# Hybrid encoder block on one core: the gated memory operand made in the values stage, small steps in PSUM, and another split of the last eight units

## The chip, the core and the metric

The kernel runs on one core of one Trainium2 chip. Its time is the device time of one execution in microseconds (us). A core has a matrix engine (TensorE, PE in the profile; PEld is its load of weights), VectorE (DVE), ScalarE (ACT), GpSimd (POOL) and SyncE (SP), which here only issues transfers between DRAM and the on-chip memory SBUF. TensorE writes its results into PSUM, a small memory of banks.

## The reference

One encoder block on 1024 tokens of width 1024, in float32. The input is normalised and multiplied by one wide matrix; its columns feed three mixers and their gates. Cut to what matters:

```python
h = rms_norm(x, g_pre)
a_qkv, bq, bk, bv, mq, ga, gb, gm, mg = split(h @ w_in)
# a: dilated window attention in three groups (windows 128, 512, 2048; dilations 1, 4, 16), 8 heads of 64 each
wts = softmax(stack(lses), axis=0)               # shares of the three groups, by their log-denominators
oa = einsum('gbsh,gbshd->bshd', wts, stack(outs))
# b: grouped attention, RMS-normalised queries and keys, rotary positions on two axes
# m: cross-attention into 256 rows of memory
om = softmax(mq @ km.T * M_HEAD_DIM ** -0.5) @ vm
ya = (oa * silu(ga)) @ w_br_a
yb = (ob * silu(gb)) @ w_br_b
ym = (om * silu(gm)) @ w_br_m
gates = sigmoid(mg + b_merge)
merged = gates[0] * ya + gates[1] * yb + gates[2] * ym
x = x + rms_norm(merged @ w_out, g_post)
```

"Operand" below means `o * silu(g)`, the left factor of one of the three branch products: 512 channels by 1024 tokens, kept as four blocks k of 128 channels, each in two halves of 512 tokens (`lo`, `hi`, `half[z]`).

## The kernel before

**Precision.** Every float32 operand of a product is split into a high part (a rounded copy, by ScalarE) and a low part (the difference, by VectorE or GpSimd); a product is then three matmuls, high·high, low·high and high·low. The helper `split` is at L105 (ScalarE's copy) and L106 (VectorE's difference). So every product needs a step of each engine ahead of it.

**Seven products for eight.** Most large products are cut into two by two blocks and made by seven block products with sums of blocks. The names A11, A12, S2, S1, S4, S3, A22 are blocks and sums on the weights' side, T1 to T4 on the tokens' side. The sum S2 needs A-blocks, S4 needs S2, S1 needs S2, and each is split before its product.

**Order of work.** Every engine runs its instructions in the order in which the program gives them; a wait holds what stands behind it on the same engine. Transfers nearly all stand in SyncE's queue in program order, so that one that waits (a store for its data, a load for its tile to come free) holds those behind it. A pool hands out tiles by name; a name with `bufs=1` has one buffer, and a new use waits for the old one's last reader.

The stages in order of time, in us of the profiled execution:

- up to 220: keys and values of the memory, attention into it. Its result o goes to `od[2]` in DRAM; the gates' silu, doubled, went to `g2d`.
- 220 to 460: the grouped attention.
- 462 to 538: products of the values stage (L1210). In its loop the eight blocks r of the b operand are made, by `operand(r, stage)`: stage 0 loads `vot` (from od), `vgt` (from g2d) and `vrt` (1/l from rld), stage 1 multiplies on VectorE (L992, L993), stage 2 stores back to od (L995). `vot` has two buffers, `vgt` and `vrt` have one.
- 538 to 579: the third group's values (L1259): 28 steps, product i and block k of step n being `divmod(n, 4)`, with 12 matmuls a step; the products run in the order A11, A12, S2, S3, S4, S1, A22; `SIDE` lists by step what the other engines do. Split S3 stands at step 8, S4 at 12, S1 at 16, the load of `tab` at 9. What remains of operand 7 is at step 7 of the list.
- 579 to 1062: 25 pairs of units (L1298), 18.3 us each: rotary parts, gates and merge gates. In the last two the memory operand is gated: `op_load` loads od and g2d halves, `op_mult` (L1323) multiplies, `op_split` splits into `hh`, `hl`.
- 1062 to 1297: `weave`. It takes turns between the dense units `y` (steps m = 0 to 15, L1862, 24 matmuls of 512 columns each: the branch products by 128 output channels) and the attention of the 12 dilated items; it hands a dense step out when the share of attention cost already given, against a total that is written in the call, is behind that of the dense work. `pend` holds small steps (evacuations, loads, splits) that are given every third dense step.
- 1297 to 1349: the last eight y units (`y_part`, L1995). `y_load` loads a weight, `y_split` splits it (ScalarE at L1337, second engine at L1338), `y_evac` multiplies the product by its merge gate (L1355, VectorE, out of PSUM) and adds it to the accumulator (L1356, GpSimd). `wo_split` splits parts of the output weights that `wo_load` brought, and `a_half` (L1982) halves the accumulators for the output product.
- 1349 to the end: the output product z (L2081), the norm and the sum with x.

The shares of the last item's three groups are made in `shares_3(T)`: from transposed rows (L1898) a minimum, differences, exponentials, a sum, a reciprocal and `parts` (L1901 to L1917), which TensorE transposes (L1922). `wide` spreads them over the channels, and `first_two` and `third` (L1946 to L1948) combine the groups' outputs; `dl_high` and `dl_low` split the result as operand of the a branch.

Of the kernel before, what the change touches and what calls it, by code (L numbers as in the profile page):

```python
# [15 lines left out]
S = 1024  # L16
# [34 lines left out]
def block(ctx: ExitStack, tc: tile.TileContext, x, xT, memT, cst, msk, bcst, tabA, gpost,  # L51
# [944 lines left out]

    turn = [0]
# [204 lines left out]
    for n in range(28):  # L1202
# [34 lines left out]
        if k == 3:  # L1237
# [3 lines left out]
            4: [lambda: v3_split("S2")], 5: [lambda: kt_split("T3", 0)], 6: [lambda: kt_split("T3", 1)], 7: [lambda: operand(7, 1), lambda: operand(7, 2)],  # L1241
# [6 lines left out]
            26: [lambda: k_block(0, "S2")], 27: [lambda: k_block(0, "S1"), lambda: k_block(0, "S3"), lambda: k_sum(0, 4)]}  # L1248
    for n in range(28):
# [59 lines left out]
    def op_load(t):  # L1309
        for k in range(4):  # L1310
            if t is lo and k % 2 == 0:
                x = vb.tile([P, 1024], F32, name=f"vA12{k // 2}")
                for z in range(2):
                    OPM[lo, k + z] = x[:, half[z]]
            elif t is hi and k % 2 == 0:
                x = vb.tile([P, 1024], F32, name=f"vA11{k // 2}")
                for z in range(2):
                    OPM[hi, k + z] = x[:, half[z]]
            for dst, src in ((tab[k // 2][:, half[k % 2]], g2d), (OPM[t, k], od)):
                nc.sync.dma_start(dst, src[2, k, :, t])  # L1320

    def op_mult(t, k):
        V.scalar_tensor_tensor(OPM[t, k], OPM[t, k], 0.5, tab[k // 2][:, half[k % 2]], op0=OP.mult, op1=OP.mult)  # L1323
# [23 lines left out]
    def y_evac(m, t, ps_):  # L1347
# [6 lines left out]
        else:  # L1354
            V.scalar_tensor_tensor(th[:, t], th[:, t], 1.0, ps_, op0=OP.add, op1=OP.mult)  # L1355
            (V if m == 23 else G).tensor_tensor(accs[f][:, t], accs[f][:, t], th[:, t], op=OP.add)  # L1356
# [15 lines left out]
    for n in range(last + 1):  # L1372
# [4 lines left out]
        k_block(n, "A22")  # L1377
        if n:
            c_fin(n - 1, 1, 1)
# [11 lines left out]
        if n == last:  # L1391
            op_split(lo, 2)
            op_split(lo, 3)
            op_load(hi)
            qk_first(0)
            th_load(0)
# [20 lines left out]
        if n == last:  # L1417
            for k in range(4):
                op_mult(hi, k)
            y_load(1)  # L1420
            qk_first(1)
# [13 lines left out]
        if n == last - 1:  # L1435
            for k in range(4):
                op_mult(lo, k)
# [9 lines left out]
    for k in range(4):  # L1447
        op_split(hi, k)
    r = RV[last, 0, 1]
# [15 lines left out]
    with ExitStack():  # L1465
# [218 lines left out]
        def plan(it, pre, nxt):  # L1684
# [7 lines left out]
            def tokens(T):  # L1692
# [7 lines left out]
                if n in (9, 10) and T == 5:  # L1700
                    dl_load(n - 9)
                if n == 11:
                    if T < 6:
                        k, z = divmod(T, 3)
                        dl_high(k, half[z]) if z < 2 else dl_low(k)
# [145 lines left out]
        def add_y(m):  # L1851
            n, i, f = steps[m]

            def gen(_):
                pend.extend([lambda: th_load(m + 1), lambda: y_load(m + 2), lambda: y_split(m + 1, G)])
# [38 lines left out]
        def shares_3(T):  # L1894
            if T == 0:
                C["ogs"] = [OG[3, x] for x in range(2)]
                tp = pst()
                PE.transpose(tp[:, 0, 0:64], rows, ident[0:64, 0:64])  # L1898
                V.tensor_copy(c3[:, 0:2].rearrange("p g h s t -> p (g h s t)"), tp[:, 0, 0:64])
                mn = cb.tile([P, 2, NT], F32, name="cmn", bufs=2)  # L1900
                V.tensor_tensor(mn, c3[:, 0, :, 0], c3[:, 1, :, 0], op=OP.min)  # L1901
                V.tensor_tensor(mn, mn, c3[:, 2, :, 0], op=OP.min)
                C["e"] = eg = cb.tile([P, 3, 2, NT], F32, name="ceg", bufs=1)
                V.tensor_tensor(eg, c3[:, :, :, 0], mn[:, None].to_broadcast([P, 3, 2, NT]), op=OP.subtract)
                A.activation(eg, eg, AF.Exp, scale=-1.0)
            elif T == 1:
                eg = C["e"]
                dn = cb.tile([P, 3, 2, NT], F32, name="cdn", bufs=1)
                V.tensor_tensor(dn, eg, c3[:, :, :, 1], op=OP.mult)
                ds_ = cb.tile([P, 2, NT], F32, name="cds", bufs=2)  # L1910
# [3 lines left out]
                V.scalar_tensor_tensor(eg, eg, 0.5, ds_[:, None].to_broadcast([P, 3, 2, NT]), op0=OP.mult, op1=OP.mult)  # L1914
                eg = eg.rearrange("p g h t -> p (g h t)")
                A.activation(parts[:, 0], eg, AF.Copy)
                V.tensor_tensor(parts[:, 1], eg, parts[:, 0].bitcast(F32), op=OP.subtract)  # L1917
                dl_high(2, lo)
            elif T == 2:
                dl_high(2, hi)  # L1920
# [3 lines left out]
                for x in range(2):  # L1924
# [3 lines left out]
                                    pick[:, None, :, None].to_broadcast([96, 32, NT, 2]), op=OP.mult)  # L1928
            else:
                dl_low(2)  # L1930
# [19 lines left out]
        def ending():  # L1950
            DL[3] = C["ogs"][0]
            return [(lambda: [wide(g, 0) for g in range(2)], 300.0), (lambda: [wide(g, 1) for g in range(2)], 300.0),
                    (lambda: [first_two(0), wide(2, 0)], 1000.0), (lambda: [first_two(1), wide(2, 1)], 1000.0),
                    (lambda: third(0), 1000.0), (lambda: dl_high(3, lo), 100.0), (lambda: third(1), 1000.0),
                    (lambda: dl_low(3, lo), 100.0), (lambda: dl_high(3, hi), 100.0), (lambda: dl_low(3, hi), 1000.0),
                    (out_pool, 100.0), (lambda: [wo_load(nm, k) for nm in ("B11", "B21") for k in range(4)], 500.0)]
# [40 lines left out]
    LATER = {16: [("B11", 0), ("B11", 1)], 17: [("B11", 2), ("B11", 3)], 18: [("B21", 0), ("B21", 1)],  # L1997
# [314 lines left out]
```

## Time and profile before

| | us |
|---|---|
| time, median of 3 runs | 1441.6 (1441.11 to 1445.11) |
| profiled execution | 1442.91 |
| its span | 1440.8 |
| granted TensorE clock, mean over the span | 0.989 |
| PE, DVE, ACT, POOL busy | 1393.1, 1024.4, 658.9, 620.7 |
| bytes moved by transfers | 208.10 MB, 144 GB/s in the mean |

The span is what the traces cover; the execution's time lies 2.1 us above it. In the profile, L12 is line 12 of the kernel; a row of the timeline gives start, length, engine, line, operation, tile written <- tiles read, shape, and in brackets the idle time of the engine ahead of it with what ended it. A count behind an x says that so many instructions are drawn together. PEclk is the granted TensorE clock as a share of full speed.

### The profile page before, as it was taken

Reading aid. Unit: us, or ns where it says so; the run is one execution under the profiler, and the core shown is the slowest. Engines: PE = TensorE matmul, PEld = TensorE weight load, DVE = VectorE, ACT = ScalarE, POOL = GpSimd, SP = SyncE. Lnnn points to the kernel's source line nnn. Section 1 sums busy time; section 2 is a strip of 40 time slices with the busy share of each in tenths; the row PEclk is TensorE's granted clock in tenths of the full one; section 3 lists DMA queues with packets and bytes.
Section 4 is the critical chain, followed back from the end, with each engine's and each line's share of the span. In section 5 each row is a group of like instructions: output and inputs, shape, how many; then the busy total and the mean of one; then the engine's idle time right before and its main releaser. Section 6 shows DMA issues by size and latency. Waiting matters only on the chain.

```text
span 1440.8 us, 21841 instructions
## 1 busy us (share of the span) xinstructions
PE 1393.1 (97%) x7775; PEld 1110.3 (77%) x7775; DVE 1024.4 (71%) x1801; ACT 658.9 (46%) x1384; POOL 620.7 (43%) x468
## 2 busy tenths in 40 slices
PE   7999999999999999999999999999989999978897
PEld 7799986666666889888888888888867777756786
DVE  7768578776763787776777766777776655665977
ACT  6544356665644444333333333333345665532332
POOL 1416703666664002354555544555510266374303
PEclk9999999999999999999999999999999999989999
DMA  6356432222111886243333333333384667744355
GB/s 239 96 168 235 161 121 88 96 77 94 59 50 45 283 265 215 76 132 102 117 104 117 117 116 111 104 102 100 114 283 159 198 211 198 219 142 148 134 205 175
DMA packets 119708, 208.10 MB, mean 144 GB/s; under 512 B 32336, under 2 KB 60848, under 8 KB 119600
## 3 DMA queue, kind: packets, MB, share of 16 engines
q1 hardware_dynamic: 109808, 192.69, 42.1%
q10 hardware_dynamic: 9792, 14.03, 2.7%
q8 instruction: 61, 1.00, 0.3%
q14 instruction: 47, 0.39, 0.1%
HBM read 142.38 MB, written 64.28 MB: 143 GB/s over the span
## 4 chain that ended last, share of the span: by engine, by line
PE 81%; DVE 6%; POOL 3%; ACT 3%; issue 3%; DMA 2%; ACTq 1%; SPq 1%; DVEq 0%; POOLq 0%
PE s L1298 32%; PE d L1862 4%; PE s L1210 4%; PE s L2081 4%; PE ov L797 3%; PE d L145 3%; PE d L143 3%; PE d L147 3%; PE s L1259 3%; PE s L1566 2%; PE s L782 2%; PE s L781 2%; PE tr L763 2%; PE tr L1638 2%; PE d L2081 2%
## 5 line engine op out<-in xcount | busy, mean ns | idle before, releaser
L788 POOL TENSOR_TENSOR bl<-bl,bp 128x512 f32<-128x512 f32 x96 | 130.8, 1362 | 54.3 <-ACT bp L784 48.9
L1298 PE MATMUL s<-hh,vS 128*128 128x512 f32 x400 | 133.6, 395 | 0.0
L1298 PE MATMUL s<-vA,vS 128*128 128x512 f32 x450 | 106.6, 390 | 0.0
L1579 ACT ACTIVATE pra<-pra,sts 128x192 f32<-128x192 f32 (+2 forms) x176 | 75.4, 430 | 54.5 <-DVE sts L1578 51.0
L106 DVE TENSOR_TENSOR vS<-vot,vS 128x512 fp32r<-128x512 f32 x75 | 85.8, 1145 | 19.9 <-ACT vS L105 19.9
L1298 PEld LDWEIGHTS s<-vA,vS 128*128 128x128 f32 x450 | 84.5, 188 | 18.3
L784 ACT ACTIVATE bp<-s 128x512 f32<-128x512 f32 x128 | 75.7, 595 | 43.6 <-PE s L782 42.6
L764 DVE TENSOR_REDUCE bn<-tr 128x1 f32<-128x512 f32 x128 | 84.8, 682 | 11.9 <-PE tr L763 10.7
L143 PE MATMUL d<-hh,wh 128*128 128x512 f32 x224 | 90.0, 402 | 2.4 <-DVE fth L216 2.4
L147 PE MATMUL d<-hh,wl 128*128 128x512 f32 x224 | 90.0, 402 | 0.0
L145 PE MATMUL d<-hl,wh 128*128 128x512 f32 x224 | 89.4, 399 | 0.0
L1298 PEld LDWEIGHTS s<-hh,vS 128*128 128x128 f32 x400 | 75.3, 188 | 18.3 <-DVE vS L106 0.4
L1298 PE MATMUL s<-hl,vS 128*128 128x512 f32 x200 | 79.1, 396 | 0.0
L1298 PE MATMUL s<-hh,wl 128*128 128x512 f32 x200 | 78.4, 392 | 0.0
L1298 PE MATMUL s<-hh,wh 128*128 128x512 f32 x200 | 78.4, 392 | 0.0
L1298 PE MATMUL s<-hl,wh 128*128 128x512 f32 x200 | 77.8, 389 | 0.0
L1617 DVE COPY app<-tr 128x384 f32<-128x384 f32 (+1 forms) x64 | 38.8, 607 | 47.8 <-PE tr L1605 31.4
L1302 ACT ACTIVATE vv<-s 128x512 f32<-128x512 f32 x50 | 29.9, 598 | 86.0 <-PE s L1298 58.1
L1356 POOL TENSOR_TENSOR acc<-acc,wl 128x512 f32<-128x512 f32 (+1 forms) x23 | 39.8, 1731 | 51.4 <-DVE wl L1355 51.3
L1338 POOL TENSOR_TENSOR wh<-wr,wh 128x512 fp32r<-128x512 f32 x20 | 26.1, 1303 | 80.2 <-ACT wh L1337 70.3
L797 PE MATMUL ov<-bp,VS 128*64 128x512 f32 x256 | 58.5, 599 | 0.0
L1044 POOL TENSOR_TENSOR vot<-vot,vA 128x512 f32<-128x512 f32 x12 | 19.0, 1583 | 91.1 <-DVE vS L106 91.1
(619 smaller groups left out, 4142.2 us busy)
## 6 DMA issues: line engine op xcount, KB each, us to landing
wr<-in_wu SPq DMA_DIRECT2D x40, 512.0 KB
vA<-in_wu SPq DMA_DIRECT2D x24, 512.0 KB
qkd<-ko SPq DMA_DIRECT2D x96, 128.0 KB
wl<-thd SPq DMA_DIRECT2D x24, 512.0 KB
wos<-os SPq DMA_DIRECT2D x12, 512.0 KB
wr<-in_wbr SPq DMA_DIRECT2D x24, 256.0 KB
aq<-qkd SPq DMA_DIRECT2D x12, 512.0 KB
ak<-qkd SPq DMA_DIRECT2D x12, 512.0 KB
```

The lines of the kernel that those rows point to most:

```text
L106: V.tensor_tensor(dst_l, src, dst_h.bitcast(F32), op=OP.subtract)
L143: PE.matmul(dst, wh[:, k, :], hh[k][:, t], start=k == 0, stop=False)
L145: PE.matmul(dst, wh[:, k, :], hl[k][:, t], start=False, stop=False)
L147: PE.matmul(dst, wl[:, k, :], hh[k][:, t], start=False, stop=k == 7)
L764: fp["last"] = V.tensor_reduce(st[i]["n"][:, j, c:c + 1], s, axis=AX.X, op=OP.min)
L784: A.activation(pp, s, AF.Exp, scale=-1.0)
L788: G.tensor_tensor(lsum[i % 2], lsum[i % 2], pp, op=OP.add)
L797: PE.matmul(o[e * 64:e * 64 + 64], VS[:, kt, kv], d.pop(kt), start=kt < 2, stop=kt >= NT - 2)
L1210: PE.matmul(now[j], a, b, start=k == 0 and q == 0, stop=k == 3 and q == 2)
L1298: PE.matmul(BANK[n, c], a, b, start=k == 0 and q == 0 and not more, stop=k == 3 and q == 2, skip_group_check=c in "XW")
L1579: A.activation(src, src, AF.Exp, scale=-1.0, bias=bias, accum_out=sts[:, h, 1, T:T + 1])
L2081: PE.matmul(dst[:, e[0]:e[1]], a, b, start=k == 0 and q == 0, stop=k == 3 and q == 2)
```

## The change

1. **Memory operand.** `memory_operand(k, stage)` makes the gated block k of the memory operand inside the L1259 loop and stores it back to `od[2]`. It uses two `vot`, one `vgt` and one `vrt`. Loads are at steps 3, 6, 9, 12, multiplications at 5, 8, 11, 14, stores at 6, 9, 12, 14. The rest of operand 7 moves to steps 2 and 3. `op_mult` and the loads of g2d in the last pair units go; the load of the second half moves one unit earlier.
2. **Last shares.** `shares_3` keeps its temporaries in a PSUM bank, sums the three terms with one tensor_reduce, and the splits `dl_high(2)`, `dl_low(2)` stand one call later.
3. **End of the attention.** LAST_PAD and the total of `weave` grow, and the last combination (`third`, `dl_high(3)`, `dl_low(3)`), `out_pool` and the loads of B11 and B21 move out of `weave` behind it, together with y_split 17 and 18 on VectorE. Units 16 to 18 are then done in k = 0, 1, next k = 2, next B11's splits, next k = 3.
4. **Last eight units.** For m from 16 on, the sum in `y_evac` and the low parts of `y_split` are on VectorE (before, the sum of m = 23 and the splits from 21 on only were).
5. Loads and splits of the first two dilated results come one item earlier.

```diff
+    def memory_operand(k, stage):
+        if stage == 0:
+            OT["m"] = [vb.tile([P, 512], F32, name=x, bufs=2 if x == "vot" else 1) for x in ("vot", "vot", "vgt", "vrt")]
+            for z in range(2):
+                for src, dst in ((od, OT["m"][z]), (g2d, OT["m"][2 + z])):
+                    nc.sync.dma_start(dst, src[2, k, :, half[z]])
+        elif stage == 1:
+            for z in range(2):
+                o, g = OT["m"][z::2]
+                V.scalar_tensor_tensor(o, o, 0.5, g, op0=OP.mult, op1=OP.mult)
+        else:
+            o = OT.pop("m")
+            for z in range(2):
+                nc.sync.dma_start(od[2, k, :, half[z]], o[z])
...
+    SIDE[2].append(lambda: operand(7, 1))
+    SIDE.setdefault(3, []).append(lambda: operand(7, 2))
+    for j in range(4):
+        for z in range(3):
+            at = min(3 + 3 * j + (0, 2, 3)[z], 14)
+            SIDE.setdefault(at, []).append(lambda j=j, z=z: memory_operand(j, z))
...
-            for dst, src in ((tab[k // 2][:, half[k % 2]], g2d), (OPM[t, k], od)):
-                nc.sync.dma_start(dst, src[2, k, :, t])
+            elif t is hi:
+                OPM[hi, k] = tab[k // 2][:, half[k % 2]]
+            nc.sync.dma_start(OPM[t, k], od[2, k, :, t])
-    def op_mult(t, k):
-        V.scalar_tensor_tensor(OPM[t, k], OPM[t, k], 0.5, tab[k // 2][:, half[k % 2]], op0=OP.mult, op1=OP.mult)
...
-            (V if m == 23 else G).tensor_tensor(accs[f][:, t], accs[f][:, t], th[:, t], op=OP.add)
+            (V if m >= 16 else G).tensor_tensor(accs[f][:, t], accs[f][:, t], th[:, t], op=OP.add)
...
     for k in range(4):
         op_split(hi, k)
+    y_split(1, G)
...
+                C["b"] = b = pss1()
+                b = b[:, 0:192].rearrange("p (x y) -> p x y", x=12)
+                C["e"] = eg = b[:, 4:7].rearrange("p g (h t) -> p g h t", h=2)
+                mn = b[:, 7].rearrange("p (h t) -> p h t", h=2)
...
-                V.tensor_tensor(ds_, dn[:, 0], dn[:, 1], op=OP.add)
-                V.tensor_tensor(ds_, ds_, dn[:, 2], op=OP.add)
+                V.tensor_reduce(ds_, b[:, 8:11].rearrange("p g x -> p x g"), axis=AX.X, op=OP.add)
...
-        weave(16, every(), FIRST_PAD + 12 * NT * (SOFT + 100.0) + 4 * LAST_PAD + 7000.0)
+        weave(16, every(), FIRST_PAD + 12 * NT * (SOFT + 100.0) + 4 * LAST_PAD + 8000.0)
         while pend:
             pend.pop(0)()
+        y_split(17)
+        y_split(18, V, qk.tile([P, S], R, name="aq", bufs=2))
+        y_load(19)
+        out_pool()
+        for nm in ("B11", "B21"):
+            for k in range(4):
+                wo_load(nm, k)
+        third(0)
+        dl_high(3, lo)
+        third(1)
+        dl_low(3, lo)
+        dl_high(3, hi)
+        dl_low(3, hi)
...
-    y_split(17, G)
-    y_split(18, G, yw.tile([P, 1024], R, name="yw"))
-    for m in range(16, 19):
-        y_part(m, range(3))
+    for ks in (range(2), range(2, 3)):
+        for m in range(16, 19):
+            y_part(m, ks)
+    for k in range(4):
+        wo_split("B11", k)
     for m in range(16, 24):
         y_part(m, range(3, 4) if m < 19 else range(4))
         if m > 16:
             y_evac(m - 1, slice(0, S), YP[m - 1].rearrange("p a b -> p (a b)"))
         if m in (16, 17):
-            y_split(m + 3, G)
+            y_split(m + 3)
...
-FIRST_PAD, LAST_PAD = 7000.0, 1000.0
+FIRST_PAD, LAST_PAD = 7000.0, 2000.0
```

More of the change, by code (lines that the diff above doesn't have):

```diff
@@ L1435, in block @@
         if n == last - 1:
[L1436 to L1437 removed]
+            op_load(hi)
         pair_product(n, "S4")
@@ L1951, in ending @@
             DL[3] = C["ogs"][0]
[L1952 to L1956, printed above, removed]
+            return [(lambda: [wide(g, 0) for g in range(2)], 500.0), (lambda: [wide(g, 1) for g in range(2)], 500.0),
+                    (lambda: [first_two(0), wide(2, 0)], 2500.0), (lambda: [first_two(1), wide(2, 1)], 2500.0)]
         def every():
```

64 lines of the change are left out of this document (27 added, 37 removed).

## The prediction

> **What bounds the kernel now.** I read the page from the top: totals, then slices, then the busy time of the stretches that the change touches, then the waits inside them.
>
> ```profile
> span 1440.8 us, 21841 instructions
> ...
> PE 1393.1 (97%) x7775; PEld 1110.3 (77%) x7775; DVE 1024.4 (71%) x1801; ACT 658.9 (46%) x1384; POOL 620.7 (43%) x468
> ...
> PE   7999999999999999999999999999989999978897
> ...
> PEclk9999999999999999999999999999999999989999
> ```
>
> TensorE is busy 97% of the span, and the change neither adds nor removes a matmul in quantity. Time can come only from the 48 us in which TensorE is idle and from stretches at a lower granted clock; time can be lost wherever TensorE is full today and something new makes it wait. The slices put nearly all gaps behind slice 29 (from about 1050 us on). The stretches, by windows (columns: window, its length, PE, PEld, DVE, ACT, POOL busy, granted clock, DMA share, GB/s):
>
> ```profile
> 538.60:578.70 40.10, 40.10 (x337) 40.10 (x336) 30.52 (x39) 17.55 (x29) 7.24 (x4) 1.00 0.68 213
> 1062.00:1082.00 20.00, 15.30 (x71) 10.37 (x69) 10.87 (x30) 8.39 (x23) 3.51 (x3) 0.91 0.91 323
> ...
> 1276.00:1286.00 10.00, 2.27 (x10) 1.50 (x10) 8.87 (x11) 0.93 (x4) 8.92 (x6) 0.79 0.38 131
> 1286.00:1297.00 11.00, 10.94 (x63) 8.68 (x64) 8.24 (x13) 2.29 (x4) 4.87 (x3) 0.72 0.51 165
> 1297.00:1321.00 24.00, 18.95 (x74) 14.46 (x72) 8.88 (x12) 6.39 (x12) 6.30 (x5) 0.93 0.40 132
> 1321.00:1349.00 28.00, 27.65 (x122) 22.93 (x123) 28.00 (x24) 10.02 (x19) 17.00 (x7) 1.00 0.50 170
> 1349.00:1362.00 13.00, 8.56 (x28) 6.33 (x27) 12.90 (x13) 1.79 (x4) 4.08 (x2) 0.74 0.24 83
> ```
>
> The first row is the third group's values loop (L1259): TensorE is never idle there, so that stretch can only get worse. The others hold the gaps, and the waits name them (what waited, on what, us, times, longest), first from 1060 to 1082, then from 1270 to 1362:
>
> ```profile
> PE d L1862 <- DVE hl L106: 2.0, 1, 2.0
> PE d L1862 <- ACT wh L1337: 1.4, 1, 1.4
> PE s L1566 <- DVE vv L1098: 0.7, 1, 0.7
> ...
> PE tr L1922 <- DVE parts L1917: 7.8, 1, 7.8
> PE d L2081 <- DVE ak L1982: 3.5, 1, 3.5
> PE sc L1995 <- POOL wh L1338: 2.6, 1, 2.6
> PE sc L1995 <- DVE wl L1355: 1.8, 1, 1.8
> ...
> PE sc L1995 <- ACT wh L1337: 1.0, 1, 1.0
> ```
>
> **Memory operand, the gain (later).** Before, the gated memory operand is multiplied by eight VectorE steps in the last pair units; the last of them waits for its load, and the split (hl L106) on which the first unit of the weave waits comes right behind it:
>
> ```profile
> 1058.91 0.42 SPq L1320 DMA_DIRECT2D vA<-od  x1
> 1064.97 0.69 DVE L1323 SCALAR_TENSOR_TENSOR vA<-vA,tab 128x512 f32<-128x512 f32 x1 [3.34 <-DMA vA<-od]
> ...
> 1066.78 1.89 DVE L106 TENSOR_TENSOR hl<-vA,hh 128x512 fp32r<-128x512 f32 x3
> ```
>
> After, the product is already in DRAM, the eight g2d loads are gone, and the four loads of the second half are issued a unit (18 us) earlier. The split waits only for product A22, which reads the tiles it overwrites; the last pair product ends where that stretch begins, at 1062, and two splits of 0.63 (1.89 for three) bring it to about 1063.5, against 1066.8 for the start of these rows. y_split(1) follows at once. The 20 us from 1062 lose 4.7 us idle and 15.3 × 0.09 = 1.4 us of clock, 6.1 in all. I take 5 (3.5 to 6): the start of the attention keeps its wait on vv.
>
> **Memory operand, the cost (earlier).** The multiplication moves into the L1259 loop: for each of four blocks two od and two g2d loads (256 KB each), two VectorE multiplications, two stores, at steps 3/5/6, 6/8/9, 9/11/12 and 12/14/14. The tiles are the ones that the values operand uses (vot with two buffers, both taken by one block; vgt and vrt with one). So nothing is double-buffered: a block's loads wait for the previous block's stores to finish, its multiplications wait for its loads, and VectorE runs in program order. Queued behind each multiplication on VectorE are the evacuations of the products, the sums S4 and S1, and the weight splits S3, S4 and S1 that TensorE needs at steps 12, 16 and 20; on SyncE, behind each store, the values' own stores, the tab loads and the next loads. Rows for the price of a round (SyncE issue, then the step that it released), and the three splits today:
>
> ```profile
> 534.12 1.16 SPq L989 DMA_DIRECT2D vrt<-rld  x2
> 539.21 0.69 DVE L993 TENSOR_TENSOR vot<-vot,vrt 128x512 f32<-128x512 f32 x1 [0.72 <-DMA vrt<-rld]
> 550.03 0.69 DVE L993 TENSOR_TENSOR vot<-vot,vrt 128x512 f32<-128x512 f32 x1
> 553.30 1.23 DVE L106 TENSOR_TENSOR wl<-vS,wh 128x1024 fp32r<-128x1024 f32 x1 [1.97 <-ACT wh L105]
> 557.47 1.23 DVE L106 TENSOR_TENSOR wl<-wr,wh 128x1024 fp32r<-128x1024 f32 x1 [0.61 <-ACT wh L105]
> 562.57 1.23 DVE L106 TENSOR_TENSOR wl<-wr,wh 128x1024 fp32r<-128x1024 f32 x1 [1.04 <-ACT wh L105]
> ...
> 657.52 0.34 ACTq L1112 DMA_DIRECT2D thd<-wh  x1
> 660.16 1.67 POOL L1044 TENSOR_TENSOR vot<-vA 128x512 f32<-128x512 f32 x1 [1.46 <-DMA thd<-wh]
> ```
>
> A store frees its tile 2.64 us after its issue (657.52 to 660.16). A load lands 3.9 us after the end of its issue (535.28 to 539.21), up to 5.6 in the row of 1058.91 (1059.33 to 1064.97); the loop's DMA share is 0.68 already. I take 3.5, a little under the first, since that one queued behind three other loads; bounds 2.9 and 4.5. Round: multiplication 0.7, store 2.64, issue of the next two loads 0.9, landing 3.5, so 7.7 us, against 3 steps × 1.43 (40.10 over 28) = 4.3. The first block: L993 of the last values operand ends at 550.7, its store then frees vot at about 553.4, two more issues 0.9, landing 3.5: multiplications at about 558. Then 565.7. The store of that second block sits on SyncE behind stores of values that come from evacuations behind the multiplication, about 3.5 more (0 to 4): 577, then 584.7. Its two multiplications and the S1 split, 1.4 + 1.2, give 587, where TensorE wants S1 at 538.6 + 20 × 1.43 = 567.2. Loss 20 us; with the short durations (7.1 a round, 1 for the queue) 15, with the long ones 25. The halved clock after a stall of some 13 us ahead of step 16 is inside it, for step 20 waits anyway. The pair units behind have nothing to make it up with: they keep TensorE full.
>
> [...]
>
> **PSUM for the last shares.** The 7.8 us wait stands behind a run of VectorE steps of 16 to 48 columns, while POOL is busy 8.92 of 10 us:
>
> ```profile
> 1243.78 0.43 DVE L1787 TENSOR_TENSOR cdn<-ceg,cpt 128x48 f32<-128x48 f32 x1
> ...
> 1276.74 1.18 DVE L1902 TENSOR_TENSOR cmn<-cmn,c 128x16 f32<-128x16 f32 x1
> 1277.95 2.30 DVE L1904 TENSOR_TENSOR ceg<-c,cmn 128x48 f32<-128x48 f32 x1
> ...
> 1280.56 1.99 DVE L1909 TENSOR_TENSOR cdn<-ceg,c 128x48 f32<-128x48 f32 x1 [0.31 <-ACT ceg L1905]
> ...
> 1285.79 0.21 DVE L1917 TENSOR_TENSOR parts<-ceg,parts 128x48 fp32r<-128x48 f32 x1 [0.31 <-ACT parts L1916]
> ...
> 1324.02 1.74 POOL L1338 TENSOR_TENSOR wh<-wr,wh 128x512 fp32r<-128x512 f32 x1
> 1324.54 1.21 DVE L1355 SCALAR_TENSOR_TENSOR wl<-wl,sc 128x1024 f32<-128x1024 f32 x1
> 1325.67 3.49 DVE L106 TENSOR_TENSOR wB<-wB 128x512 fp32r<-128x512 f32 x2
> 1325.83 2.78 POOL L1356 TENSOR_TENSOR acc<-acc,wl 128x1024 f32<-128x1024 f32 x1
> ...
> 1334.22 1.28 DVE L106 TENSOR_TENSOR wT<-wT 128x512 fp32r<-128x512 f32 x2
> ```
>
> The same 48-column step takes 0.43 at 1243.78 and 1.99 to 2.30 beside POOL: two operands in SBUF stretch to the end of the POOL step. L1355 at 1324.54 has one operand in PSUM, lies inside a POOL step, and takes 1.21 us; the pair of splits at 1325.67, all SBUF, takes 3.49 beside POOL and 1.28 without. With one operand in PSUM the chain, today 9.1 us (1276.74 to 1285.8), falls to about 3.2 (ten steps of 0.2 to 0.4 and their handovers), and a dozen matmuls of 0.23 and transposes lie under that. Gone: 7.8 us of wait and 11 × 0.28 = 3.1 us of low clock behind it; against it a remaining wait of 0 to 3. I take 9 (7 to 11). [...]
>
> **Two units kept, VectorE alone.** From 1297 to 1321 TensorE loses 5.05 us idle and 18.95 × 0.07 = 1.3 of clock: its waits are on the splits of weights (ACT 1.0, POOL 2.6) and on an evacuation (1.8). After, y_split(17) and y_split(18) are on VectorE right behind the weave, and the third group's last combination stands under units 16 to 18 instead of in front of them: I take 5 of 6.3 (2 to 6). From 1349 to 1362 it loses 4.44 idle and 8.56 × 0.26 = 2.2 of clock, because VectorE, 28.00 of 28.00 busy before, comes late with ak. Without POOL's steps a split pair costs 1.28 instead of 3.49: five pairs save 11 us. Added are seven sums of 1.22 (a 1024-column step at 1.23) and four weight splits of 0.68, 11.3 us. So VectorE gains nothing in sum but starts earlier (B11 before the last parts), and its 4.5 to 5.7 us a unit stands against 24 matmuls × 0.23 (27.65 over 122) = 5.5. I take 6 of 6.6 (2 to 7). Small rest, dilated loads an item earlier and a new pace of units: +1 (-1 to 2).
>
> **Sum.** 5 + 9 + 5 + 6 + 1 = 26 gained (21 to 31 when not all ends fall together), 20 lost (15 to 25): 6 us less. The profiled execution took 1442.9 (span 1440.8 and 2.1 around it), 1.3 over the median of 1441.6: 1436.9, and 1435.6 as a median.
>
> **Rivals.** *Slower:* the rounds are longer. Price: with landings of 5.6 us, as at 1064.97, a round is 9.8 and the loss 2.1 + 3 × 2.1 more, 28; with the gains at 21 that is +7, 1449. It decides from a loss of about 30 at full gains or 25 at low ones. For it: the loop's other transfers, four serial rounds; against it: the share of 0.68 leaves room. *A balance:* a new wait at the end takes the place of those removed (y_split(18) waits for its load, or the first parts for rows), and the last two terms give 5 instead of 11: 1441.6. For it: VectorE's sum is unchanged there. It also covers that fewer than two units are left at the end of the items. *Short rounds:* no queue on SyncE and landings of 2.9 or less, so a loss of 11: 1426.6.
>
> **Numbers.** What a measurement of this kernel can tell from no change is 0.3%, 4.3 us. Chances: forecast 0.42, of it 0.36 below 1437.3 and 0.06 above; balance 0.18, of it 0.15 within and 0.03 slower; slower 0.22; short rounds 0.18. Faster 0.54, same 0.21, slower 0.25. The range reaches from the low side of the short rounds' middle to the slower case: 1423 to 1449. The forecast's own is 1430 to 1440.
>
> **What would show it.** Right: in the L1259 loop TensorE idle some 20 us in waits on the weight splits, VectorE idle there on DMA into vot, vgt or vrt; the wait on parts under 2 us; VectorE's split pairs at 1.28 in the last units; the wait on hl gone or under 0.5. Wrong: no TensorE wait in that loop, or over 28 us of it; VectorE still full from the end of the items on, with TensorE waiting for it by as much as before.

## The result and the profile after

| | before | after |
|---|---|---|
| median of 17 runs each, us | 1442.25 (1440.59 to 1445.11) | 1446.35 (1444.73 to 1451.96) |
| ratio to before | | 1.0032 (95% interval 1.0023 to 1.0040) |
| profiled span, us | 1440.8 | 1444.5 |

The change made the kernel 4.1 us slower, where 6 us less had been forecast. The head of the page after (totals, slices, granted clock):

```profile
span 1444.5 us, 21871 instructions
...
PE 1392.9 (96%) x7775; PEld 1112.6 (77%) x7775; DVE 1012.0 (70%) x1811; ACT 659.6 (46%) x1384; POOL 596.2 (41%) x457
...
PE   8999999999999996799999999999999999998997
...
PEclk9999999999999998899999999999999999999999
```

The dip has moved. Before, TensorE's low slices stood behind slice 29; now they are slices 16 and 17, which were full. The stretches show the same (third group's loop, stretch of the last shares, first part and rest of the last eight units):

```profile
539.30:605.40 66.10, 46.14 (x337) 45.09 (x337) 34.40 (x47) 16.88 (x27) 6.25 (x4) 0.85 0.71 219
...
1288.00:1298.00 10.00, 8.77 (x67) 6.63 (x67) 4.80 (x19) 5.86 (x24) 9.92 (x6) 1.00 0.48 144
...
1306.40:1321.00 14.60, 8.82 (x28) 6.64 (x28) 10.57 (x16) 4.67 (x8) 3.32 (x3) 0.77 0.76 250
1321.00:1359.40 38.40, 37.80 (x167) 30.97 (x166) 29.22 (x35) 12.13 (x22) 0.00 (x0) 1.00 0.56 186
```

The loop's 337 matmuls took 40.1 us and take 66.1. Between equal points of the two traces:

| from the first matmul of ... to that of ... | before | after | difference |
|---|---|---|---|
| third group's loop, to the weave | 524.0 | 549.5 | +25.5 |
| weave, to unit 16 | 234.7 | 217.8 | -17.0 |
| unit 16, to the second product of z | 64.0 | 58.4 | -5.6 |
| second product of z, to the end | 79.7 | 79.7 | 0.0 |

With 0.8 us ahead of the loop, where nothing is changed, that is the 3.7 us between the spans. The longest waits of TensorE over the whole trace (us, times, longest):

```profile
PE s L1281 <- DVE wl L106: 15.3, 4, 13.0
...
PE sc L2023 <- ACT hh L1859: 5.8, 1, 5.8
PE s L1281 <- ACT wh L105: 4.6, 1, 4.6
...
PE d L1879 <- POOL wh L1354: 1.5, 1, 1.5
```

Two new waits stand there, 19.9 us in the loop and 5.8 behind unit 16; of before, the waits on parts, hl, vv, aq and ak are gone.

**The loop.** SyncE's timeline and, under it, VectorE's from the second to the third block of the memory operand, and the two matmuls that waited longest (start, length, engine, line, tiles, idle ahead of it):

```profile
562.01 7.39 SPq L1186 DMA_DIRECT2D vdr<-vv  x4
569.44 1.00 SPq L1258 DMA_DIRECT2D tab<-in_tabA  x2
570.48 0.91 SPq L1011 DMA_DIRECT2D od<-vot  x2
576.51 0.32 SPq L1003 DMA_DIRECT2D vot<-od  x1
...
563.45 0.69 DVE L1007 SCALAR_TENSOR_TENSOR vot<-vot,vgt 128x512 f32<-128x512 f32 x1
566.62 0.69 DVE L1007 SCALAR_TENSOR_TENSOR vot<-vot,vrt 128x512 f32<-128x512 f32 x1 [2.48 <-DMA vrt<-g2d]
...
580.63 0.69 DVE L1007 SCALAR_TENSOR_TENSOR vot<-vot,vgt 128x512 f32<-128x512 f32 x1 [11.59 <-DMA vgt<-g2d]
582.66 0.69 DVE L1007 SCALAR_TENSOR_TENSOR vot<-vot,vrt 128x512 f32<-128x512 f32 x1 [1.34 <-DMA vrt<-g2d]
...
583.87 1.22 DVE L106 TENSOR_TENSOR wl<-wr,wh 128x1024 fp32r<-128x1024 f32 x1
...
562.32 0.53 PE L1281 MATMUL s<-wh,vA 128*128 128x256 f32 x2 [4.64 <-ACT wh L105]
...
585.14 0.58 PE L1281 MATMUL s<-wl,hh 128*128 128x256 f32 x1 [12.99 <-DVE wl L106]
```

Read it backwards: TensorE waited 13.0 us for S4's low part (583.87), which stood on VectorE behind two multiplications, which waited 11.6 us for the loads of 576.51, which waited for the store of 570.48 to free its tiles, and that store stood on SyncE behind the stores of values (562.0 to 569.4) and 1 MB of tab loads. The round from 563.45 to 580.63 took 17.2 us. The wait of 4.6 us at 562.32, for S3's high part, has the same origin: ScalarE's copy stood behind a scaling of values, this behind an evacuation by VectorE, and that behind the first block's multiplications (556.07 and 558.44).

**The end.** ScalarE's and VectorE's timeline behind the first twelve matmuls of unit 16:

```profile
1310.41 0.63 ACT L1353 ACTIVATE wh<-wr 128x512 fp32r<-128x512 f32 x1 [5.88 <-DMA wr<-in_wbr]
1311.00 0.63 ACT L1353 ACTIVATE aq<-wr 128x512 fp32r<-128x512 f32 x1
1311.07 0.69 DVE L1354 TENSOR_TENSOR wh<-wr,wh 128x512 fp32r<-128x512 f32 x1 [3.15 <-ACT wh L1353]
1311.68 0.68 DVE L1354 TENSOR_TENSOR aq<-wr,aq 128x512 fp32r<-128x512 f32 x1
...
1314.34 0.68 DVE L1964 TENSOR_TENSOR og<-tr,og 128x512 f32<-128x512 f32 x1
...
1315.17 0.77 PE L2023 MATMUL sc<-hh,wh 128*128 128x512 f32 x1 [5.78 <-ACT hh L1859]
```

The view names ScalarE's hh, but in the program the first matmul of unit 17 waits for its split of ScalarE and for the step of `third` (L1964) that reads the last of the PSUM tile whose bank unit 17 takes over; that step ends at 1315.02. It stands on VectorE behind y_split 17 and 18, and these wait for a weight load.

### The profile page after: what moved, and what is told of

It reads as the page before. It is cut to its first block, busy times and chain, and to the rows that moved or that the text cites. A ratio compares the mean times of both kernels' runs of the same rounds, so it can differ in the third digit from the quotient of the medians.

```text
span 1444.5 us, 21871 instructions
## 1 busy us (share of the span) xinstructions
PE 1392.9 (96%) x7775; PEld 1112.6 (77%) x7775; DVE 1012.0 (70%) x1811; ACT 659.6 (46%) x1384; POOL 596.2 (41%) x457
## 4 chain that ended last, share of the span: by engine, by line
PE 80%; DMA 6%; DVE 4%; POOL 3%; ACT 3%; issue 3%; SPq 1%; ACTq 0%; DVEq 0%; POOLq 0%
PE s L1320 33%; PE s L2105 4%; PE d L1879 4%; PE s L1226 4%; PE ov L797 3%; PE sc L2023 3%; PE d L145 3%; PE d L143 3%; PE d L147 3%; PE s L782 2%; PE s L781 2%; PE tr L763 2%; PE d L2105 2%; PE s L1580 1%; PE tr L1652 1%
## 5 line engine op out<-in xcount | busy, mean ns | idle before, releaser
L1320 PE MATMUL s<-hh,vS 128*128 128x512 f32 x400 | 133.4, 395 | 0.0
L1320 PE MATMUL s<-vA,vS 128*128 128x512 f32 x450 | 106.6, 390 | 0.0
L1320 PEld LDWEIGHTS s<-vA,vS 128*128 128x128 f32 x450 | 84.5, 188 | 18.3
L1320 PEld LDWEIGHTS s<-hh,vS 128*128 128x128 f32 x400 | 75.3, 188 | 17.7
L1320 PE MATMUL s<-hl,vS 128*128 128x512 f32 x200 | 79.1, 395 | 0.0
L1320 PE MATMUL s<-hh,wh 128*128 128x512 f32 x200 | 78.4, 392 | 0.0
L1320 PE MATMUL s<-hh,wl 128*128 128x512 f32 x200 | 78.4, 392 | 0.0
L1320 PE MATMUL s<-hl,wh 128*128 128x512 f32 x200 | 77.8, 389 | 0.0
L143 PEld LDWEIGHTS d<-hh,wh 128*128 128x128 f32 x224 | 42.6, 190 | 16.3 <-issue 5.5
L1592 DVE CUSTOM_DVE_ANT_0 pra<-s,mask 128x192 f32<-128x192 f32 (+2 forms) x192 | 53.9, 323 | 1.1 <-PE s L1580 1.1
```

The source lines that it names most:

```text
L143: PE.matmul(dst, wh[:, k, :], hh[k][:, t], start=k == 0, stop=False)
L1320: PE.matmul(BANK[n, c], a, b, start=k == 0 and q == 0 and not more, stop=k == 3 and q == 2, skip_group_check=c in "XW")
```

## The experiments

Times are medians; "ratio" is to runs of the kernel before on the same chip, with its 95% interval.

**e1: the operand late.** All of the change but the memory operand:

```diff
+            4: [lambda: v3_split("S2")], 5: [lambda: kt_split("T3", 0)], 6: [lambda: kt_split("T3", 1)], 7: [lambda: operand(7, 1), lambda: operand(7, 2)],
...
-    SIDE[2].append(lambda: operand(7, 1))
...
-            SIDE.setdefault(at, []).append(lambda j=j, z=z: memory_operand(j, z))
...
+                op_mult(hi, k)
```

> The changed kernel with the memory operand made as before (eight multiplications and the g2d loads in the last pair units, rest of the values operand at step 7), all other parts as changed. Theory A (the loop's chain of loads, multiplications and stores costs about 26 us and the early operand brings 4 to 6 us at the start of the weave): 1446.4 - 26 + 5 = 1425 us, no TensorE wait in the third group's values loop, the wait on hl back. Theory B (most of the loss is only moved: without the chain the pair units or the weave would wait as long): 1440 or above. Theory C (the other parts bring nothing, the end's new wait of 5.8 us takes all): about 1442.

1429.05 us, ratio 0.9903 (0.9889 to 0.9916), 4 above A's figure and far from B's and C's. The operand costs 17 us in all, the rest brings 13: the loss is not moved, it is made in the loop, where TensorE no longer waits. The wait on hl is back (2.6), the one behind unit 16 stays (5.4).

**e2: the operand only.** The other way round, on the kernel before.

```diff
+    for j in range(4):
+        for z in range(3):
+            at = min(3 + 3 * j + (0, 2, 3)[z], 14)
+            SIDE.setdefault(at, []).append(lambda j=j, z=z: memory_operand(j, z))
...
-                op_mult(hi, k)
```

> The kernel before with the memory operand made in the values stage, and nothing else of the change. Theory A: 1442.2 + 26 - 5 = 1463 us (1458 to 1468), with the same TensorE waits in the loop as in the changed kernel (13 us ahead of S4's low part). Theory B: within 5 us of 1442. If the start of the weave brings nothing: 1468.

1462.54 us, ratio 1.0135 (1.0120 to 1.0150), 20 us more than before, with a longest wait of 13.4 us in the loop. From both sides the operand costs 17 to 20 us net. The loop is 25.2 us longer than before here, and 26.0 shorter in e1 than in the changed kernel; the weave gives 7.4 and 10.9 of that back.

**e3: the tab loads behind the chain.**

```diff
-            8: [lambda: v3_split("S3")], 9: [lambda: [nc.sync.dma_start(tab[j], tabA[:, j]) for j in range(2)]],
-            11: [lambda: G.tensor_tensor(tab[1], tab[1], rb, op=OP.mult)], 17: [lambda: V.tensor_tensor(tab[0], tab[0], rb, op=OP.mult)],
+            8: [lambda: v3_split("S3")], 15: [lambda: [nc.sync.dma_start(tab[j], tabA[:, j]) for j in range(2)]],
+            17: [lambda: G.tensor_tensor(tab[1], tab[1], rb, op=OP.mult)], 21: [lambda: V.tensor_tensor(tab[0], tab[0], rb, op=OP.mult)],
```

> The changed kernel with the two tab loads (1 MB) at step 15 instead of 9, behind the chain's last store, and their multiplications at 17 and 21. If the third round is long because its store and loads stand behind 1 MB of tab loads: the store frees its tiles in about 3 us instead of 5.6, the 11.6 us wait of VectorE falls to 7 or less, and the time by 4 to 6 us, to 1441. If the round is long because SyncE stands at the stores of the values (562.0 to 569.4): within 1.5 us of 1446.4. If the late tab holds the pair units: slower than 1448.

1443.01 us, ratio 1.0005 (0.9994 to 1.0016): 3.3 us less than the changed kernel, a little under the 4 to 6 expected. The loop is 4.8 us shorter (61.3 against 66.1), and 1.7 of that is lost again in the pair units. The third block's rows:

```profile
568.61 1.00 SPq L1011 DMA_DIRECT2D od<-vot  x2
570.88 0.32 SPq L1003 DMA_DIRECT2D vot<-od  x1
...
575.44 0.69 DVE L1007 SCALAR_TENSOR_TENSOR vot<-vot,vgt 128x512 f32<-128x512 f32 x1 [7.23 <-DMA vgt<-g2d]
```

The first tile is free 2.3 us behind the start of the stores, where it was 6.0 behind 1 MB of tab loads, and VectorE's wait falls from 11.6 to 7.2. That is the part of the mis-sized round that the tab loads made.

**e4: the last combination first.**

```diff
+        third(0)
+        dl_high(3, lo)
+        third(1)
         y_split(17)
         y_split(18, V, qk.tile([P, S], R, name="aq", bufs=2))
...
-                pend.extend([lambda: th_load(m + 1), lambda: y_load(m + 2)])
+                pend.extend([lambda: y_load(m + 2), lambda: th_load(m + 1)])
```

> The changed kernel with the last combination (third, first half of dl_high(3)) ahead of y_split 17 and 18 in the order of VectorE and ScalarE, and with y_load(m+2) ahead of th_load(m+1) on SyncE. If the 5.8 us wait after unit 16's first matmuls comes from VectorE, held by the weight load of y_split(18) (5.88 us idle on ScalarE for wr) in front of the step that frees the PSUM bank: wait under 2 us, low clock gone, 1439 to 1441 us. If TensorE really waited for hh (ScalarE): the same or 1 to 2 us less. If the loads alone are late: the wait stays, now on the split of unit 17.

1444.78 us, ratio 1.0011 (1.0000 to 1.0022), 1.6 us less; the expected 5 to 7 did not come. By the time alone that is the second case. But the wait behind unit 16 fell from 5.8 to 2.8 us and is now for ScalarE's part of y_split(17), which this order put behind dl_high(3) and its wait for VectorE: the edit may have moved the wait rather than missed it. e8 takes that up.

**e5: the operand spread.** Two blocks at the head of the values loop before, two in the third group's loop behind the splits S4 and S1:

```diff
+            elif at == 0 and r in (-2, -1) and n >= 0:
+                memory_operand(r + 2, stage)
...
+    SIDE[3].append(lambda: memory_operand(2, 0))
+    SIDE[12].append(lambda: memory_operand(2, 1))
+    SIDE[13][:0] = [lambda: memory_operand(2, 2), lambda: memory_operand(3, 0)]
+    SIDE[16].append(lambda: memory_operand(3, 1))
+    SIDE[17].append(lambda: memory_operand(3, 2))
```

> The changed kernel with the four memory blocks placed otherwise: two ahead of the eight blocks of the b operand in the values loop before (same three-step spacing, whose steps are 2.7 us there), two in the third group's loop with their multiplications behind the splits S4 (step 12) and S1 (step 16), the tiles of the sums SF taken at step 18 instead of 15. Theory A (what costs is that VectorE and SyncE are held in front of splits that TensorE needs, as rounds of 8 us stand in 4.3 us): no wait over 1 us in the loop, and the gain at the start of the weave stays: 1446.4 - 24 = 1420 to 1424 us, below the run with the operand made late (1429.1). Rival (the loads and stores themselves, 4 MB more beside the values' transfers, hold TensorE): 1430 or above.

1438.57 us, ratio 0.9972 (0.9958 to 0.9986), in the rival's numbers. The waits on VectorE's splits, in the earlier loop and in the third group's, tell the two halves of the edit apart:

```profile
PE s L1226 <- DVE wl L106: 8.2, 1, 8.2
...
PE s L1284 <- DVE wl L106: 1.5, 2, 0.9
```

The two blocks behind the splits that TensorE needs next cause waits of 1.5 us, and make the loop 2.1 and the pair units 1.7 us longer; the two at the head cause a wait of 8.2, and the loop begins 11 us later than before. SyncE issued their loads only behind eight weight loads (465.2 to 474.4), they landed at 481, and VectorE stood still for 9.0 us in front of a split. So it is A's mechanism, VectorE held in front of a split, at a place that I had taken for free; what held it are late loads, which is the rival's part.

**e6: the shares in PSUM only.** The new shares_3 in the kernel before:

```diff
-                mn = cb.tile([P, 2, NT], F32, name="cmn", bufs=2)
+                C["b"] = b = pss1()
+                mn = b[:, 7].rearrange("p (h t) -> p h t", h=2)
```

> The kernel before with the last shares' temporaries in PSUM (and its splits dl_high(2), dl_low(2) one call later), nothing else. By my sum 9 us less: 1433 (1431 to 1436), the wait on parts from 7.7 to under 1 us. If the PSUM operand is not what frees the steps (POOL stretches them all the same, or TensorE's clock stays low for another reason): 1440 or above. If the wait is only taken over by the next one at the end (POOL wh, ScalarE): 1437 to 1440.

1437.45 us, ratio 0.9979 (0.9964 to 0.9994): 3.7 us less, not 9, which is the third case. (Between the profiled executions the weave is 6.0 us shorter; the runs lie between 1434.5 and 1443.3.) The steps are as short as expected, and the wait on parts is 0.7 us; but this is what TensorE waits for 4.6 us later, when the gap on parts no longer hides it:

```profile
1276.26 0.32 PE L1921 MATMUL tr<-cs,parts 128*96 128x128 f32 x1 [0.70 <-DVE parts L1918]
...
1280.87 0.79 PE L1862 MATMUL d<-bh,wh 128*128 128x512 f32 x1 [3.83 <-POOL wh L1338]
```

**e7: VectorE alone only.**

```diff
-            (V if m == 23 else G).tensor_tensor(accs[f][:, t], accs[f][:, t], th[:, t], op=OP.add)
+            (V if m >= 16 else G).tensor_tensor(accs[f][:, t], accs[f][:, t], th[:, t], op=OP.add)
...
-    y_split(17, G)
+    y_split(17)
```

> The kernel before with the sums of y_evac for m from 16 on and the weight splits 17 to 20 on VectorE instead of GpSimd, nothing else. By my sum the split pairs fall from 3.5 to 1.3 us and seven sums of 1.22 and four splits come on top, so VectorE's sum is about even: 1441 to 1443 with the waits on aq and ak at 1351 and 1356 of about the same length; the waits on POOL wh (2.6) and on wl (1.8) go, 2 to 4 us. If GpSimd's stretching was the greater part: 1436 or below. If VectorE becomes the bound: above 1444.

1430.74 us, ratio 0.9919 (0.9899 to 0.9940): 10.4 us less, below even the lowest of my three cases. From unit 16 to the second product of z, first before, then e7:

```profile
1297.10:1361.10 64.00, 54.17 (x217) 42.90 (x216) 48.77 (x46) 17.52 (x32) 27.39 (x13) 0.92 0.42 140
...
1296.30:1349.30 53.00, 50.05 (x218) 40.33 (x217) 43.90 (x55) 17.63 (x32) 2.96 (x2) 1.00 0.49 169
```

VectorE does more instructions and is busy 5 us less; the waits on POOL wh, wl, aq and ak are all gone, and the clock stays full.

**e8: spread, with the end mended.** As e5, with y_load first as in e4, and y_split(17), next the two steps that free the bank, then the rest:

```diff
         y_split(17)
+        for zt, zx in zip(half, range(2)):
+            V.tensor_tensor(zb[:, zt], W3B[2, zx], zb[:, zt], op=OP.mult)
+        third_rest(0)
         y_split(18, V, qk.tile([P, S], R, name="aq", bufs=2))
...
-        third(0)
         dl_high(3, lo)
-        third(1)
+        third_rest(1)
```

> The spread placement, and at the end: y_load(m+2) ahead of th_load(m+1) on SyncE, y_split(17) first, then the two steps that free the PSUM bank of the third share, then the rest, with y_split(18) behind. Theory: the wait of 5.8 us after unit 16's first half and its low clock go as well: 4 to 7 us below the spread placement alone, 1415 to 1419 us. If the bank was not what TensorE waited for: within 2 us of the spread placement.

1431.34 us, ratio 0.9919 (0.9898 to 0.9940), 7.2 below e5; the 1415 to 1419 expected was reckoned from a better e5 and missed with it. The matmul behind unit 16's first half now names the step that frees the bank:

```profile
1298.95 0.47 PE L2035 MATMUL sc<-hh,wh 128*128 128x512 f32 x1 [0.97 <-DVE og L1989]
```

So the bank was what TensorE waited for, and the end's order was worth 7 us.

**e9: spread later.** The first two blocks of e8 as four half blocks in two tiles of their own:

```diff
+    SIDE[4].append(lambda: memory_half(0, 0, 0))
+    SIDE[12].append(lambda: memory_half(0, 0, 1))
+    SIDE[13][1:1] = [lambda: memory_half(0, 0, 2)]
+    SIDE[13].append(lambda: memory_half(0, 1, 0))
+    SIDE[16].append(lambda: memory_half(0, 1, 1))
...
+    SIDE[27].append(lambda: memory_half(1, 1, 1))
```

> As the spread placement with the mended end, but the first two memory blocks are taken out of the head of the earlier values loop (where TensorE waited 8.2 us for a split behind them) and made as four half blocks in two tiles of their own in the third group's loop: loads at steps 4, 13, 18, 23, multiplications at 12, 16, 22, 27, each behind the split of its step. Theory A (only the place on VectorE ahead of splits costs): 8 us of wait and 4 of low clock go, 1418 to 1422 us. Rival (the loop's DMA share, then near 1, makes the loads too late for these steps): waits of 5 us or more in the loop, 1425 to 1432.

1429.78 us, ratio 0.9900 (0.9884 to 0.9916): the rival. The waits on splits in the loop are 7.8 us: the multiplications of step 16 waited for loads up to 576.8, while the split of A22 stood behind them.

**e10: the multiplications on GpSimd.**

```diff
-                V.scalar_tensor_tensor(o, o, 0.5, g, op0=OP.mult, op1=OP.mult)
+                G.tensor_tensor(o, o, g, op=OP.mult)
```

> The changed kernel with the eight multiplications on GpSimd instead of VectorE (same steps, same loads, stores and tiles; the factor 0.5 goes into op_split). If VectorE held in front of S3, S4 and S1 is what costs: the waits on wl in the loop fall under 3 us in all, and what is left is a wait at the start of the pair units, as their sums and loads stand behind the chain on GpSimd and SyncE: 1430 to 1440. If the transfers or SyncE's order cost by themselves: still 1443 or above.

1444.02 us, ratio 1.0013 (0.9999 to 1.0027), 2.3 us less than the changed kernel, whose interval it meets: the second case. The waits at the loop (L1281) and at the start of the pair units (L1320):

```profile
PE s L1320 <- ACT wh L105: 6.0, 1, 6.0
...
PE s L1320 <- ACT vv L1324: 4.6, 1, 4.6
PE s L1281 <- DVE wl L106: 3.6, 2, 2.1
```

VectorE no longer holds the splits (3.6 us instead of 15.3), and almost the same time is lost one stage later: the loop is 20.4 us shorter than in the changed kernel and the pair units 16.5 longer, where the first weights stand on SyncE behind the chain. What costs is the length of the chain, some 40 us of rounds one behind the other; in this run the engine that multiplies only decided who waits for it.

**e11: two parts.** e6 and e7 together, on the kernel before:

```diff
+                C["b"] = b = pss1()
...
+            (V if m >= 16 else G).tensor_tensor(accs[f][:, t], accs[f][:, t], th[:, t], op=OP.add)
```

> The kernel before with the last shares in PSUM and VectorE alone in the last eight units, and nothing else. Alone they gave -4 and -10 us. If they add up and the other parts of the end (units kept, third behind the weave, dilated loads earlier) bring nothing or a loss: 1426 to 1429, the same as or below the run with the operand late (1429). If the kept units bring the 5 us of my sum: 1431 or above here.

1426.01 us, ratio 0.9881 (0.9865 to 0.9898), 17 us less: they add up (3.7 and 10.4 are 14.1; the interval begins at 14.7). It lies 3 us below e1, with intervals that meet, so the other parts of the end, as the change has them, bring no gain; that they lose is likely, but not shown by the times.

**e12: two parts and the late spread.** e11 with e9's operand and, among others, these edits against e11:

```diff
+    y_split(1, G)
     r = RV[last, 0, 1]
...
+                pend.extend([lambda: y_load(m + 2), lambda: th_load(m + 1)])
```

> The kernel of the two parts (shares in PSUM, VectorE alone) with the memory operand in the late spread placement, the early y_split(1), and y_load ahead of th_load; without the end's new order. The start of the weave brings 6 us: 1420 to 1423, against 1418 to 1422 for the late spread with the mended end. If the mended end is worth its 5 us: 4 to 6 us above that one.

1438.59 us, ratio 0.9973 (0.9962 to 0.9984), 16 us above the expectation and 12.6 above e11: 11.9 us of waits at the loop and the first pair unit, 4.8 on POOL wh in the weave, and a low clock (0.75) at 1280 to 1300 again. Against e11 the loop is 10.8 us longer and the pair units 4.8, and the weave only 3.5 shorter: the early operand is worth less in this surrounding than its chain costs.

**e13: the operand late, the end mended.** e1 with the end of e8:

```diff
-                pend.extend([lambda: th_load(m + 1), lambda: y_load(m + 2)])
+                pend.extend([lambda: y_load(m + 2), lambda: th_load(m + 1)])
...
         y_split(17)
+            V.tensor_tensor(zb[:, zt], W3B[2, zx], zb[:, zt], op=OP.mult)
+        third_rest(0)
         y_split(18, V, qk.tile([P, S], R, name="aq", bufs=2))
```

> The changed kernel without its memory operand part (made late, as before) and with the mended end (y_load ahead of th_load; y_split(17), then the two steps that free the third share's PSUM bank, then the rest, with y_split(18) behind). If the two faults are independent and together account for the miss: 1429 - 7 = 1422 us (0.986 of the kernel before), the wait of 5.4 us behind unit 16 down to about 1, and less than the two parts alone (1426). If the kept units bring nothing even so: 1426. If the late operand's own waits eat the gain: 1429.

1419.45 us, ratio 0.9829 (0.9809 to 0.9848): 24 us less than before, 27 less than the changed kernel, below every other version. Its page:

```profile
PE 1386.4 (98%) x7775; PEld 1105.0 (78%) x7775; DVE 1013.0 (71%) x1811; ACT 659.3 (46%) x1384; POOL 599.2 (42%) x457
...
PE   7999999999999999999999999999999999999997
```

No slice between the first and the last is under 90% now. The time is 2.5 us under the 1422 expected of two independent faults. Against e1 the last units are 6.2 us shorter and the weave 4.7, where the waits on POOL wh fall from 4.3 to 1.2; the same end brought 7.2 over e5, nearly all of it in the last units. And with the same end the late operand is 10 to 12 us better than the two spread ones (e8, e9): no place for the early operand that was tried here paid.

## Why the prediction was wrong

**Cost of the operand in the loop: mechanism right, size too small.** The forecast was 20 (15 to 25), the stretches give 26.0. The chain began as worked out: first multiplications at 556.1 and 563.5 (forecast 558 and 565.7). The step that failed is the price of the later rounds, and most of it is one store: the third round has 7.7 + 3.5 = 11.2 us in the sum and 17.2 in the trace. The wait of the store in SyncE's queue was right (567.3 to 570.5, 3.2 us), but I gave the store 2.64 us, and here it took 6.0 behind 1 MB of tab loads; I had named those loads as queued *behind* the chain and had not priced them ahead of it. e3, without those loads ahead, took 3.8 us off the store, and its loop loses 21.2 us, close to the 20. So the tab loads are 4.8 of the 6.0 us that were missing. (The row of the 2.64 does not show what I read in it: the GpSimd step at 660.16 neither reads nor writes the tile `wh` that was stored. The size was near the 2.3 of e3 all the same.)

The rest lies in the second halves of the blocks. I had put both multiplications of a block behind one landing. But the second half's loads wait for the second store, and they landed 3.3 to 5.3 us behind the end of their issue, where the first halves' took 2.8 to 3.5. In the second block this is a wait of 2.48 us, and in the fourth of 3.39, right in front of S1's split, where the loss ends:

```profile
591.52 0.69 DVE L1007 SCALAR_TENSOR_TENSOR vot<-vot,vrt 128x512 f32<-128x512 f32 x1 [3.39 <-DMA vrt<-g2d]
...
592.73 1.22 DVE L106 TENSOR_TENSOR wl<-wr,wh 128x1024 fp32r<-128x1024 f32 x1
...
594.00 0.39 PE L1281 MATMUL s<-wl,vA 128*128 128x256 f32 x1 [0.75 <-DVE wl L106]
```

That split ends at 593.95, where the sum had 587; from 594.0 on the loop runs at full clock without a wait. The low clock was rightly put inside the term: it was 0.50 from 585.1 to 590.0 (as before behind the 7.8 us wait, from 1286.0 to 1292.0), and TensorE still had to wait 0.75 us for S1, so a full clock would only have made that wait longer.

**Gain at the start of the weave: the waits right, the gain too small.** The waits on hl, vv and wh are gone, and the first 20 us, which lost 6.1, lose nothing (TensorE is busy for 20.0 at full clock). The whole weave takes 234.7 us before, 227.3 with the operand alone (e2), 228.7 with all but the operand (e1) and 217.8 with both: the operand brings 7.4 to 10.9 us there, against 5 (3.5 to 6). Some of it comes later in the weave, where the waits on POOL wh are 1.5 us in the changed kernel and 4.3 in e1; what shortened them was not followed up.

**Shares in PSUM: the mechanism right, the gain alone too high.** Steps of 16 to 48 columns beside POOL, in the changed kernel:

```profile
1294.08 1.28 POOL L1372 TENSOR_TENSOR acc<-acc,wl 128x512 f32<-128x512 f32 x1
...
1294.33 0.21 DVE L1922 TENSOR_TENSOR s<-c,s 128x48 f32<-128x48 f32 x1
1294.80 0.22 DVE L1927 TENSOR_TENSOR s<-s,c 128x48 f32<-128x48 f32 x1 [0.26 <-ACT s L1923]
```

Before, they stood beside these:

```profile
1277.84 2.35 POOL L1806 TENSOR_TENSOR og<-og,wgt 128x1024 f32<-128x1024 f32 x1
1280.14 2.35 POOL L1849 TENSOR_TENSOR hl<-hl,hh 128x1024 fp32r<-128x1024 f32 x1
```

They take 0.21 and 0.22 where they took 2.30 and 1.99 and ended with the GpSimd steps, at 1280.25 and 1282.55; the chain takes 2.7 us (1293.63 to 1296.28). At 48 columns a step took 0.21 us with an operand in PSUM (1294.33) and 0.21 with both in SBUF and no GpSimd step beside it (before, 1285.79). But alone the edit brought 3.7 us, not 9 (e6): I had priced the wait that goes without asking what is late next. The weave as a whole is 17.0 us shorter, against 15 for my three terms there (5, 9 and 1), and that this is so near is luck: e6 and e1 both have a weave of 228.7, 6.0 less than before, so the shares bring 6.0 of their 9, pacing and earlier loads nothing that shows, and the operand more than its 5.

**VectorE alone: sized wrongly.** "VectorE gains nothing in sum" was the step that failed. I had counted five split pairs, 11 us, against seven sums and four splits. VectorE's splits of the output weights in the same stretch, first before, then e7 (busy, mean ns, idle ahead):

```profile
L106 DVE TENSOR_TENSOR wB<-wB 128x512 fp32r<-128x512 f32 x8 | 12.4, 1592 | 14.9 <-ACT wB L105 14.9
L106 DVE TENSOR_TENSOR wT<-wT 128x512 fp32r<-128x512 f32 x8 | 11.8, 1503 | 0.0
...
L106 DVE TENSOR_TENSOR wT<-wT 128x512 fp32r<-128x512 f32 x8 | 5.2, 684 | 0.0
L106 DVE TENSOR_TENSOR wB<-wB 128x512 fp32r<-128x512 f32 x8 | 5.2, 685 | 0.0
```

All but the pair at 1334.22 (1.28 us) and the last single split (0.68 at 1352.57) had been stretched: 24.2 us became 10.4, and two halvings (ak) fell from 3.5 to 1.4. So 15.9 us were saved where the sum had 11, and VectorE's busy time falls by 5.

**Units kept: a new wait took the place of the old ones.** I took 11 us for the last two terms and named "y_split(18) waits for its load" as the rival that takes them. From unit 16 to the second product of z it is 64.0 us before and 53.0 in e7, whose edit holds the splits 17 and 18 too: VectorE alone brings the whole 11. The changed kernel has 58.4, so its kept units took 5.4 of that back, with the wait of 5.8 and a clock of 0.77; in e13 it is 51.2. What I had not seen is that unit 17's PSUM tile takes over the bank that the third share leaves: the order of two engines alone does not show it.

**The sum.** 25.5 lost, 22.6 gained, 0.8 ahead of it all: +3.7 in the spans, where the sum had 20 and 26. So some 6 us of the miss are the chain and 3 the gains. The slower rival had the right place and came true near the lower of its two points, a loss of 25 with low gains, though more by a queue in front of a store than by long landings; the balance rival came true beside it. No run shows the short rounds' loss of 11: the landings in the changed kernel were 2.8 to 5.3 us, and even without the tab loads ahead (e3) the loop lost 21.2.

## What to carry to other kernels

A pattern of load, multiply, store with single buffers has a length of its own (here 7 to 17 us a round); count the time of the loop steps it is put into, and what stands in the same transfer queue ahead of each store. Where a step is moved, it is the chain's length that has to be hidden: in e10 giving the work to an idle engine only moved the wait (the loop 20.4 us shorter, the pair units 16.5 longer). Price a stall that goes by what is late next, and look at who frees the PSUM bank, not only at data, when work is reordered.

## What the runs showed of the hardware

VectorE steps with two operands in SBUF were stretched to the end of a GpSimd step beside them: five of the last shares' steps ended within 0.06 us of one, and those of 48 columns took 2.30 and 1.99 us, where 0.21 was enough with no GpSimd step beside them (1285.28, 1285.79); the one of 0.43 at 1243.78 ended 0.06 us behind a GpSimd step too. With one operand in PSUM they took 0.21 and 0.22 inside a GpSimd step. It showed over a whole stage: with GpSimd's 24 us taken out of the last units (27.39 to 2.96), VectorE had more instructions and 5 us less busy time. A store whose tile was free in 2.3 us took 6.0 with 1 MB of loads issued just ahead of it on the same queue, and 7.0 in e10, where they stood ahead as well.
